# RWKV chain: block-diagonal keys instead of block-diagonal states, one state updated in place, w2/a2 products ordered by kind, v transposed on the full array

## The chip, the cores and the metric

The kernel runs on one core of one Trainium2 chip. The core has a matrix engine (TensorE, PE in the profile, with its weight loads as PEld), a vector engine (DVE), a scalar engine (ACT), GpSimd (POOL) and a queue engine (SP) that issues most DMAs. Each engine works through its own instructions in order and waits on semaphores for the others. The metric is device time in microseconds, a median of runs of one launch.

## The reference, cut to what matters

The model has two layers of a first kind on 256 tokens and 256 context tokens, and one hybrid layer. Each layer of the first kind holds an RWKV branch, a convolution branch, gates, and a product-key expert layer. The change lies in the RWKV branch, which for 16 heads of width 64 and both directions computes

```
def step(S, inp):                       # S: 64x64 state of a head
    w_t, k_t, v_t, kk_t, a_t = inp[:5]
    sa = jnp.einsum('bhvk,bhk->bhv', S, kk_t)
    S = (S * w_t[:, :, None, :] - sa[..., None] * (kk_t * a_t)[:, :, None, :]
         + v_t[..., None] * k_t[:, :, None, :])
    y = jnp.einsum('bhvk,bhk->bhv', S, inp[5]) if emit else None
    return S, y
```

with decay `w` from `tanh(w1) @ w2[d]` and `a` from `a1 @ a2[d]`, where w2 and a2 have 64 rows for each direction d. In layer 0 outputs are wanted for all 512 tokens; in layer 1 only for the 256 that aren't context.

## The kernel before, in words

Activations lie channels by tokens; a pair of heads fills the 128 partitions. Each layer walks over 8 pairs, 16 in all. For a pair, `rwkv_a` projects k, r and v (128 channels x 512 tokens), forms the w2 and a2 products of both directions (weights 64 x 128, tile `w2` with direction 0 in partitions 0 to 63 and direction 1 in 64 to 127; L432 and L437), scans the decay, and builds for each of 8 chunks of 64 tokens the chunk matrices (`scps`, L485), the transposed keys (`btps`, L499) and the tile `uv`, whose upper 64 partitions hold the chunk's v with tokens on partitions (`vps`, L509, and its copies, L511). `rwkv_inv` inverts the chunks' triangular matrices, mostly on DVE, with 32x32 matmuls (L678, L684 in layer 0; L742 to L772 in layer 1).

`rwkv_b` is the chain: 8 steps for each direction, one chunk a step. A step is `bp` (L571, plus L573 with the state `zb` and the keys `krp`), two copies of its head blocks to `bs` (L578, one on DVE, one on ACT), `up` (L580), two copies to `uv` (L582), `zp` (L585), and the new state: ACT scales the old state by `pcs` into the other of two buffers (L589), and DVE adds `zp`, head block by head block (L592). States are block-diagonal, 64x64 for each head; the keys are written twice side by side by a copy on GpSimd (L569), so that one product serves both heads. Outputs `yp` (L557) are one product with the state and, a step later, one with `uv`.

The instruction order on each engine is not the program's order: a scheduler at build time, with priorities and a cost model of its own, sorts the instructions, and fills the chain's gaps on PE with independent projections (`zbps`, `zaps`, `gtps`, `zps`, L258, and `adaps`, L279), as the table `PLAN` hands them out. The work of pair j in `rwkv_a` and the chain of pair j-1 run interleaved. PSUM tiles of the tag `rk` come from two buffers, which the w2 and a2 products, `scps`, `btps` and `vps` share.

## Time and profile before

| | before |
|---|---|
| median of 3 runs | 5218.21 us (5210.64 to 5221.29) |
| profiled execution, device time | 5211.48 us |
| its span, first to last instruction | 5209.7 us |
| PE busy | 4967.9 us, 95% |
| DVE busy | 3488.0 us, 67% |
| ACT busy | 2561.0 us, 49% |
| POOL busy | 182.2 us, 3% |
| chain that ended last | PE 74%, ACT 12%, DVE 8%, DMA 3% |

The pairs of layer 0 run from about 90 to 1010 us of the span, those of layer 1 from about 2930 to 3640 us; the change touches nothing outside them. A PE record counts as busy until its modelled end, so short waits between matmuls are hidden in the busy share; they show as the distance between starts. An fp32 matmul leaves two records (two passes), a PE transpose one.

### The profile page before, as it was taken

Reading aid. Unit: us, or ns where it says so; the run is one execution under the profiler, and the core shown is the slowest. Engines: PE = TensorE matmul, PEld = TensorE weight load, DVE = VectorE, ACT = ScalarE, POOL = GpSimd, SP = SyncE. Lnnn points to the kernel's source line nnn. Section 1 sums busy time; section 2 is a strip of 40 time slices with the busy share of each in tenths; the row PEclk is TensorE's granted clock in tenths of the full one; section 3 lists DMA queues with packets and bytes.
Section 4 is the critical chain, followed back from the end, with each engine's and each line's share of the span. In section 5 each row is a group of like instructions: output and inputs, shape, how many; then the busy total and the mean of one; then the engine's idle time right before and its main releaser. Section 6 shows DMA issues by size and latency. Waiting matters only on the chain.

```text
span 5209.7 us, 86462 instructions
## 1 busy us (share of the span) xinstructions
PE 4967.9 (95%) x33298; PEld 4170.8 (80%) x33298; DVE 3488.0 (67%) x7830; ACT 2561.0 (49%) x4754; POOL 182.2 (3%) x409
## 2 busy tenths in 40 slices
PE   8999998999999999999999999998899999989989
PEld 6677776678777888888887787877889999987888
DVE  4888878558995455555555566656796777765654
ACT  4345444534989322222223445445478544455564
POOL 0000001000000000000000010101000000000000
PEclk9999999999999999999999899888999999999999
DMA  4332323543444644444442332323656877733544
GB/s 137 107 91 88 90 81 93 167 151 101 160 171 163 234 144 142 142 143 142 143 146 70 111 84 78 85 61 92 210 187 222 279 227 238 226 116 118 167 131 146
DMA packets 432974, 740.50 MB, mean 142 GB/s; under 512 B 132210, under 2 KB 273202, under 8 KB 427826
## 3 DMA queue, kind: packets, MB, share of 16 engines
q1 hardware_dynamic: 431042, 732.29, 44.1%
q8 instruction: 262, 4.29, 0.3%
q10 hardware_dynamic: 1520, 2.69, 0.1%
q14 instruction: 150, 1.23, 0.1%
HBM read 622.37 MB, written 112.49 MB: 141 GB/s over the span
## 4 chain that ended last, share of the span: by engine, by line
PE 74%; ACT 12%; DVE 8%; DMA 3%; issue 2%; SPq 0%; ACTq 0%; POOL 0%; DVEq 0%; POOLq 0%
PE v L1180 20%; PE s L258 14%; PE zps L258 5%; ACT ws L1126 3%; PE adaps L279 3%; PE qps L258 2%; PE ops L258 2%; PE gtps L258 2%; ACT pt L1121 2%; PE ops L1368 2%; ACT whi L238 2%; ACT pt L1120 2%; PE bp L571 1%; DVE wlo L240 1%; PE zbps L258 1%
## 5 line engine op out<-in xcount | busy, mean ns | idle before, releaser
L258 PE MATMUL s<-h,whi 128*128 128x512 f32 (+1 forms) x4096 | 1058.7, 343 | 1.3 <-ACT whi L238 0.7
L240 DVE TENSOR_TENSOR wlo<-wraw,whi 128x1024 fp32r<-128x1024 f32 (+2 forms) x602 | 724.7, 1205 | 470.9 <-ACT whi L238 458.4
L238 ACT CAST whi<-wraw 128x1024 fp32r<-128x1024 f32 (+2 forms) x602 | 621.9, 1034 | 727.0 <-PE s L258 200.0
L258 PEld LDWEIGHTS s<-h,whi 128*128 128x128 f32 x4096 | 703.8, 191 | 68.6 <-ACT ge L1136 1.0
L258 PE MATMUL s<-h,wlo 128*128 128x512 f32 (+1 forms) x2048 | 704.2, 344 | 9.1 <-DVE wlo L240 9.1
L1180 PE MATMUL v<-al,vh 128*128 128x512 f32 (+1 forms) x2048 | 689.7, 337 | 0.6 <-DVE al L953 0.6
L1180 PE MATMUL v<-ah,vl 128*128 128x512 f32 (+1 forms) x2048 | 689.2, 337 | 0.0
L1180 PE MATMUL v<-ah,vh 128*128 128x512 f32 (+1 forms) x2048 | 682.7, 338 | 2.1 <-ACT ah L952 1.5
L952 ACT CAST vh<-vraw 128x1024 fp32r<-128x1024 f32 x256 | 261.9, 1050 | 719.2 <-PE v L1180 574.9
L1226 DVE SCALAR_TENSOR_TENSOR x<-v,mod,x 128x256 f32<-128x256 f32 x768 | 333.7, 477 | 272.6 <-PE v L1180 272.1
L1180 PEld LDWEIGHTS v<-ah,vh 128*128 128x128 f32 x2048 | 387.3, 190 | 49.7 <-ACT ah L952 9.4
L1180 PEld LDWEIGHTS v<-al,vh 128*128 128x128 f32 x2048 | 388.8, 190 | 46.3 <-DVE al L953 4.8
L258 PEld LDWEIGHTS s<-h,wlo 128*128 128x128 f32 x2048 | 390.3, 191 | 44.4 <-DVE wlo L240 10.3
L1180 PEld LDWEIGHTS v<-ah,vl 128*128 128x128 f32 x2048 | 388.1, 190 | 40.3 <-issue 1.4
L953 DVE TENSOR_TENSOR vl<-vraw,vh 128x1024 fp32r<-128x1024 f32 x256 | 308.6, 1220 | 98.9 <-ACT vh L952 98.9
L258 PE MATMUL zps<-h,whi 128*128 128x512 f32 (+3 forms) x896 | 293.6, 407 | 15.5 <-DVE lz L363 7.5
L1125 PEld LDWEIGHTS wps<-qt,pt 128*128 128x128 f32 x1536 | 215.8, 190 | 109.5 <-ACT pt L1121 91.2
L1125 PE MATMUL wps<-qt,pt 128*128 128x128 f32 x1536 | 272.3, 292 | 22.2 <-ACT pt L1121 13.6
L1126 ACT COPY ws<-wps 128x512 f32<-128x512 f32 x192 | 210.5, 1097 | 5.7 <-PE wps L1125 5.2
L258 PEld LDWEIGHTS zps<-h,whi 128*128 128x128 f32 (+1 forms) x896 | 167.5, 198 | 52.8 <-issue 16.6
L279 PE MATMUL adaps<-adaw,cs 128*2 128x128 f32 x1536 | 202.0, 274 | 5.4 <-DMA adaw<-ada 3.2
L1121 ACT ACTIVATE pt<-pt,tr,tr 128x128 f32<-128x128 f32 x384 | 180.4, 489 | 2.5
(614 smaller groups left out, 9617.4 us busy)
## 6 DMA issues: line engine op xcount, KB each, us to landing
wraw<-peu SPq DMA_DIRECT2D x256, 512.0 KB, 4.2
vraw<-pev SPq DMA_DIRECT2D x256, 512.0 KB, 4.5
wraw<-win SPq DMA_DIRECT2D x139, 512.0 KB, 3.6
adaw<-ada SPq DMA_DIRECT2D x96, 512.0 KB, 3.6
wd<-ws SPq DMA_DIRECT2D x24, 2048.0 KB, 6.8
wt<-wd SPq DMA_DIRECT2D x32, 1024.0 KB, 6.8
wraw<-w_q SPq DMA_DIRECT2D x32, 512.0 KB, 3.7
gd<-ge SPq DMA_DIRECT2D x64, 256.0 KB, 2.1
```

The costliest lines, as they stand in the source:

```text
L238: nc.scalar.copy(hi, raw)
L240: nc.vector.tensor_sub(lo, raw, hi.bitcast(F32))
L258: nc.tensor.matmul(out, w[wi][:, k, :], a[ai][:, k, ts], start=n == 0, stop=n == 3 * ko - 1)
L279: nc.tensor.matmul(ps[0:2, i * P:i * P + P], self.cs[:, k, :], w[:, k, :], start=k == 0, stop=k == KO - 1)
L952: self.nc.scalar.copy(hi, src)
L953: self.nc.vector.tensor_sub(lo, src, hi.bitcast(F32))
L1120: nc.scalar.activation(pt, self.iota, AF.Abs, bias=tr[3][:, cs])
L1121: nc.scalar.activation(pt, pt, AF.Relu, bias=tr[2][:, cs], scale=tr[4][:, cs])
L1125: nc.tensor.matmul(ps[:, t, :], pt, qt[:, t1 + t], start=True, stop=True)
L1126: nc.scalar.copy(ws[:, :, t0 + t1:t0 + t1 + 4].rearrange("p i t -> p t i"), ps)
L1180: nc.tensor.matmul(ps[:, m, :], va[i][wi][:, ms], aa[i][ai], start=n == 0, stop=n == 3 * GI - 1)
L1226: nc.vector.scalar_tensor_tensor(x[:, k, ts], src[:, m, ts], self.mod[l][:, 40 + k, s:s + 1], x[:, k, ts], op0=ALU.mult, op1=ALU.add)
```

## The change

Four edits, in `rwkv_a` and `rwkv_b`:

- The two w2 products (directions 0 and 1) are written one after the other, then their two activations, then the same for a2. Before it was w2, a2 of direction 0, then of direction 1.
- v is transposed with four 128x128 transposes into one PSUM tile, two chunks in each, instead of eight products of 64 columns into two tiles. Four copies to `uv` remain, each of 64 x 512 elements.
- `krp` is now block-diagonal and holds keys and receptances (2 x 2 x 64). Two GpSimd copies a step and direction write it (one for each head) instead of one. Both `bp` and the output product read it.
- The state is a full 128x128 tile, one for each direction, whose off-diagonal blocks are never read into a result. ACT scales it in place, and DVE adds `zp` in one instruction of 128x128 instead of two of 64x64.

```diff
--- before.py
+++ after.py
@@ -426,18 +426,16 @@
         pcs = rp.tile([P, 2, 8], F32, tag="pcs", name="pcs", bufs=2)
         t65 = lambda name: rp.tile([P, 8, 65], F32, tag="t65", name=name, bufs=2)
         lds, ths, bes = [], [], []
-        for d in range(2):
-            ds = slice(64 * d, 64 * d + 64)
-            ps = pr.tile([P, 512], F32, tag="rk", name="wps")
-            nc.tensor.matmul(ps, w2[ds, 0], self.tw[ds], start=True, stop=True)
-            ld = tl("ld")
-            nc.scalar.activation(ld, ps, AF.Tanh, scale=0.5, bias=self.w0h[:, d, j:j + 1])
-            lds.append(ld)
-            ps = pr.tile([P, 512], F32, tag="rk", name="aps")
-            nc.tensor.matmul(ps, w2[ds, 1], self.za[ds], start=True, stop=True)
-            th = tl("th")
-            nc.scalar.activation(th, ps, AF.Tanh, scale=0.5, bias=self.a0h[:, d, j:j + 1])
-            ths.append(th)
+
+        for q, (src, bias, res, name) in enumerate(((self.tw, self.w0h, lds, "ld"), (self.za, self.a0h, ths, "th"))):
+            pss = [pr.tile([P, 512], F32, tag="rk", name=("wps", "aps")[q]) for _ in range(2)]
+            for d in range(2):
+                ds = slice(64 * d, 64 * d + 64)
+                nc.tensor.matmul(pss[d], w2[ds, q], src[ds], start=True, stop=True)
+            for d in range(2):
+                t = tl(name)
+                nc.scalar.activation(t, pss[d], AF.Tanh, scale=0.5, bias=bias[:, d, j:j + 1])
+                res.append(t)
         self.pop("z")
         for d in range(2):
             ld, th = lds[d], ths[d]
@@ -503,12 +501,13 @@
             nc.gpsimd.memset(uv[0:64], 0.0)
             UV.append(uv)
         self.pop("t")
-        for c0 in range(0, 8, 4):
-            ps = pr.tile([P, 4, P], F32, tag="rk", name="vps")
-            for c in range(4):
-                nc.tensor.matmul(ps[64:128, c, :], v[:, (c0 + c) * 64:(c0 + c) * 64 + 64], self.ident, start=True, stop=True)
-            for d in range(2):
-                nc.scalar.copy(UV[d][64:128, c0:c0 + 4, :], ps[64:128])
+
+        ps = pr.tile([P, 4, P], F32, tag="rk", name="vps")
+        for c in range(4):
+            nc.tensor.transpose(ps[:, c, :], v[:, c * P:c * P + P], self.ident)
+        for d in range(2):
+            for e in range(2):
+                nc.scalar.copy(UV[d].rearrange("p (c e) m -> p c e m", e=2)[64:128, :, e], ps[64 * e:64 * e + 64])
         bo = tl("bo", "bo", 2)
         nc.vector.tensor_add(bo[:, :Tr], kds[0][:, :Tr], kds[1][:, :Tr])
         nc.vector.scalar_tensor_tensor(bo[:, :Tr], bo[:, :Tr], self.par(l, "r_k", j), r[:, :Tr], op0=ALU.mult,
@@ -534,11 +533,13 @@
         if self.bs is None:
             tiles = lambda name, n: [[rp.tile([P, P], F32, name=f"{name}{d}{i}", bufs=1) for i in range(n)] for d in range(2)]
 
-            self.bs, self.zb, self.krp = tiles("bs", 1), tiles("zb", 2), tiles("krp", 1)
+
+
+            self.bs, self.zb = tiles("bs", 1), tiles("zb", 1)
+            self.krp = [rp.tile([P, 2, 2, 64], F32, name=f"krp{d}", bufs=1) for d in range(2)]
             for d in range(2):
                 nc.gpsimd.memset(self.bs[d][0][64:128], 0.0)
-                for t in self.zb[d]:
-                    nc.gpsimd.memset(t, 0.0)
+                nc.gpsimd.memset(self.krp[d], 0.0)
         oT = rp.tile([P, T2], F32, tag="oT", name="oT", bufs=1)
 
 
@@ -565,14 +566,15 @@
                 Z = Zs[d]
                 bp = ch(d, "bp")
                 if i:
-                    krp = self.krp[d][0]
-                    nc.gpsimd.tensor_copy(krp.rearrange("p (h t) -> p h t", h=2),
-                                          KR[d][:, 0, c * 64:c * 64 + 64].unsqueeze(1).to_broadcast([P, 2, 64]))
+                    krp = self.krp[d]
+                    n = 2 if emit(c) else 1
+                    for hh, hs in enumerate(heads):
+                        nc.gpsimd.tensor_copy(krp[hs, 0:n, hh], KR[d][hs, 0:n, c * 64:c * 64 + 64])
                 nc.tensor.matmul(bp, SC[d](c, 0), UV[d][:, c, :], start=True, stop=i == 0)
                 if i:
-                    nc.tensor.matmul(bp, krp, Z, start=False, stop=True)
+                    nc.tensor.matmul(bp, krp[:, 0].rearrange("p h t -> p (h t)"), Z, start=False, stop=True)
                     if emit(c):
-                        output(c, Z, KR[d][:, 1, c * 64:c * 64 + 64].unsqueeze(1).to_broadcast([P, 2, 64]))
+                        output(c, Z, krp[:, 1])
                 bs = self.bs[d][0]
                 for hh, hs in enumerate(heads):
                     copy[hh](bs[0:64, hs], bp[hs, hs])
@@ -583,15 +585,13 @@
                 if i < 7 or l == 0:
                     zp = ch(d, "zp")
                     nc.tensor.matmul(zp, BT[d][:, c, :], UV[d][:, c, :], start=True, stop=True)
-                    zn = self.zb[d][i % 2]
+                    zn = self.zb[d][0]
                     pc = pcs[:, d, c:c + 1]
                     if i:
                         nc.scalar.activation(zn, Z, AF.Copy, scale=pc)
-                    for hs in heads:
-                        if i:
-                            nc.vector.scalar_tensor_tensor(zn[hs, hs], zp[hs, hs], pc[hs], zn[hs, hs], op0=ALU.mult, op1=ALU.add)
-                        else:
-                            nc.vector.tensor_scalar(zn[hs, hs], zp[hs, hs], pc[hs], None, op0=ALU.mult)
+                        nc.vector.scalar_tensor_tensor(zn, zp, pc, zn, op0=ALU.mult, op1=ALU.add)
+                    else:
+                        nc.vector.tensor_scalar(zn, zp, pc, None, op0=ALU.mult)
                     Zs[d] = zn
                 if late[d]:
                     output(*late[d])
```

What the scheduler makes of it, at three places. First PE at the front of the second pair of layer 0, where the w2 products are `wps<-tw` and the a2 products `aps<-za`, direction 0 before direction 1. Before:

```order
L417 MATMUL ssps<-sq,blk 128x512
L432 MATMUL wps<-tw,w_1359 128x512
L580 MATMUL up<-bs_1815,sc 128x128
L437 MATMUL aps<-za,w_1359 128x512
L432 MATMUL wps<-tw,w_1359 128x512
L571 MATMUL bp<-uv,sc 128x128
L258 MATMUL gtps<-h_119,wlo 128x512
```

Now:

```order
L417 MATMUL ssps<-sq,blk 128x512
L434 MATMUL wps<-tw,w_1354 128x512
L582 MATMUL up<-bs_1805,sc 128x128
L434 MATMUL wps<-tw,w_1354 128x512
L434 MATMUL aps<-za,w_1354 128x512
L573 MATMUL bp<-uv,sc 128x128
```

The second w2 product has moved ahead of the first a2 product. Before, the adjacent pair was a2 of direction 0 with w2 of direction 1; now it is w2 of direction 1 with a2 of direction 0. Over the 16 pairs, products of opposite directions stood next to each other 10 times before, and do 8 times now.

Second PE in the chain that runs beside the third pair of layer 0; the two directions are told apart by the buffers of `bs` and of `zb` and `krp`. Before:

```order
L580 MATMUL up<-bs_1815,sc 128x128
L279 MATMUL adaps<-adaw,cs 2x128
L571 MATMUL bp<-uv,sc 128x128
L573 MATMUL bp<-zb_1820,krp_1822 128x128
L585 MATMUL zp<-uv,bt 128x128
L557 MATMUL yp<-kr,zb_1820 128x128
L557 MATMUL yp<-sc,uv 128x128
L580 MATMUL up<-bs_1816,sc 128x128
```

Now:

```order
L573 MATMUL bp<-uv,sc 128x128
L575 MATMUL bp<-zb_1807,krp_1809 128x128
L558 MATMUL yp<-krp_1809,zb_1807 128x128
L558 MATMUL yp<-sc,uv 128x128
L573 MATMUL bp<-uv,sc 128x128
L575 MATMUL bp<-zb_1808,krp_1810 128x128
L582 MATMUL up<-bs_1805,sc 128x128
L558 MATMUL yp<-krp_1810,zb_1808 128x128
L558 MATMUL yp<-sc,uv 128x128
L582 MATMUL up<-bs_1806,sc 128x128
L279 MATMUL adaps<-adaw,cs 2x128
L587 MATMUL zp<-uv,bt 128x128
```

Before, the directions took turns half a step apart: `bp` of one stood beside `zp` of the other. Now they go in step, both `bp`, both `up`, both `zp`.

Third ACT at the same place, with the in-place scale `zb<-zb`. Before:

```order
L578 COPY bs_1815<-bp 64x64
L582 COPY uv<-up 64x64
L578 COPY bs_1816<-bp 64x64
L589 ACTIVATE zb_1817<-zb_1818,pcs 128x128
L582 COPY uv<-up 64x64
```

Now:

```order
L591 ACTIVATE zb_1807<-zb_1807,pcs 128x128
L580 COPY bs_1805<-bp 64x64
L580 COPY bs_1806<-bp 64x64
L591 ACTIVATE zb_1808<-zb_1808,pcs 128x128
L584 COPY uv<-up 64x64 x2
```

The scale of direction 0 now stands ahead of the copy to `bs`, and that of direction 1 ahead of both copies to `uv`; being in place, each waits for the output product that reads the state. ACT also loads its function tables 125 times in the whole program now, 113 before; 10 of the 12 more stand among the decay's activations of layer 1, at L420 (rn) and L437 (ld, th).

## Rows read from the trace of the kernel before

**Rows 1.** First part of the page: busy time, share of the span, instructions.
```profile
PE 4967.9 (95%) x33298; PEld 4170.8 (80%) x33298; DVE 3488.0 (67%) x7830; ACT 2561.0 (49%) x4754; POOL 182.2 (3%) x409
```

**Rows 2.** Busy time by stretch; last columns PE clock, DMA share, GB/s.
```profile
200.00:800.00 600.00, 586.00 (x3896) 434.91 (x3895) 489.71 (x1283) 288.74 (x617) 55.89 (x135) 0.99 0.30 89
800.00:1010.00 210.00, 188.70 (x1154) 134.70 (x1153) 150.25 (x361) 107.38 (x224) 25.32 (x40) 0.93 0.35 109
2930.00:3500.00 570.00, 551.23 (x5742) 459.69 (x5741) 367.33 (x1009) 274.47 (x629) 58.56 (x140) 0.89 0.29 81
```

**Rows 3.** Groups by line and shape: the products that transpose v.
```profile
L509 PE MATMUL vps<-ident,v 128*64 128x128 f32 x256 | 34.8, 279 | 1.1 <-ACT bt L500 1.1
```

**Rows 4.** Timeline of PE, layer 0: start, duration, instruction, records merged.
```profile
253.19 1.09 PE L509 MATMUL vps<-ident,v 128*64 128x128 f32 x8
254.21 0.49 PE L557 MATMUL yp<-sc,uv 128*128 128x128 f32 x2
```

**Rows 5.** Timeline of PE, layer 0: four transposes among chain matmuls.
```profile
327.76 0.39 PE L573 MATMUL bp<-zb,krp 128*128 128x128 f32 x2
327.98 0.61 PE L499 MATMUL btps<-ident,be 128*128 128x128 f32 x4
328.43 0.39 PE L557 MATMUL yp<-kr,zb 128*128 128x128 f32 x2
```

**Rows 6.** Timeline of PE, first pair: a2 and w2 products, adjacent and alone.
```profile
94.50 0.69 PE L437 MATMUL aps<-za,w 64*128 64x512 f32 x1
94.50 0.69 PE L432 MATMUL wps<-tw,w 64*128 64x512 f32 x1
...
95.56 0.50 PE L258 MATMUL zbps<-h,wlo 128*128 128x512 f32 x1
...
98.50 1.12 PE L437 MATMUL aps<-za,w 64*128 64x512 f32 x2
```

**Rows 7.** Timeline of all engines, one chain step of layer 0.
```profile
331.46 0.39 PE L573 MATMUL bp<-zb,krp 128*128 128x128 f32 x2
...
332.19 0.21 ACT L578 COPY bs<-bp 64x64 f32<-64x64 f32 x1 [0.75 <-DVE bs L578]
...
332.45 0.49 PE L580 MATMUL up<-bs,sc 128*128 128x128 f32 x2
...
333.22 0.21 ACT L582 COPY uv<-up 64x64 f32<-64x64 f32 x1
...
333.72 0.39 PE L585 MATMUL zp<-uv,bt 128*128 128x128 f32 x2
...
334.17 0.58 DVE L592 SCALAR_TENSOR_TENSOR zb<-zp,pcs,zb 64x64 f32<-64x64 f32 x2
...
335.54 0.39 PE L573 MATMUL bp<-zb,krp 128*128 128x128 f32 x2
```

**Rows 8.** Groups by line and shape: state update, a wider update, the scale.
```profile
L592 DVE SCALAR_TENSOR_TENSOR zb<-zp,pcs,zb 64x64 f32<-64x64 f32 x416 | 117.5, 282 | 41.9 <-PE zp L585 32.3
L1226 DVE SCALAR_TENSOR_TENSOR x<-v,mod,x 128x256 f32<-128x256 f32 x768 | 333.7, 477 | 272.6 <-PE v L1180 272.1
L589 ACT ACTIVATE zb<-zb,pcs 128x128 f32<-128x128 f32 x208 | 82.8, 401 | 133.7 <-DVE zb L592 126.6 <-DVE zb L594 3.3 <-DVE tm L720 2.6
```

**Rows 9.** Waits of PE, 800 to 1010 us: total us, times, longest.
```profile
PE bp L571 <- DVE zb L592: 9.1, 9, 2.7
```

**Rows 10.** Groups of ACT: table loads in the decay (count, busy, mean ns).
```profile
L439 ACT ACT_TABLE_LOAD x10 | 12.8, 1283 | 0.2
```

**Rows 11.** The GpSimd key copy: durations (min/median/max), and its group.
```profile
L569 POOL COPY krp<-kr x224: 288/293/1266, 101.7 to 3621.8; 128x128 f32<-128x128 f32 x112
...
L569 POOL COPY krp<-kr 128x128 f32<-128x128 f32 x224 | 87.7, 391 | 633.0 <-PE bp L573 628.4 <-DMA am<-inv 2.9 <-DVE kr L464 1.8
```

**Rows 12.** Busy time by stretch around the inversion of a layer-1 pair.
```profile
3214.00:3220.00 6.00, 5.09 (x261) 4.53 (x259) 1.87 (x4) 2.79 (x9) 0.09 (x1) 1.00 0.02 5
3220.00:3226.00 6.00, 6.00 (x96) 5.23 (x97) 3.19 (x8) 2.28 (x4) 0.86 (x1) 0.54 0.01 3
```

## The prediction

> **What bounds the kernel now.** I read the page's first part, then the busy time by stretch, then PE's timeline inside a stretch. PE is busy 95% of the span [rows 1], and 586 of 600 us while layer 0's pairs run, 551 of 570 in layer 1's [rows 2]; only the last chain of layer 0, where projections run out, leaves 21 of 210 us open. DVE is next with 490 of 600. So in these stretches PE work that goes away shortens the kernel about one for one, DVE, ACT and POOL work only where PE waits for it. The busy share hides short waits, though: in the chain the reader must look at the distance between starts. A chain step goes from the `bp` product at 331.46 to that direction's next at 335.54, 4.08 us, and the directions share it [rows 7]. Matmuls back to back start 0.22 us apart (327.76 to 327.98, [rows 5]). In a step PE has 12 chain products and two fillers, 14 x 0.22 = 3.1 us; the other 1.0 us of the step is waiting that no view shows as idle.
>
> **v transposed on the full array.** 256 records of `vps` [rows 3] are 128 products in 32 groups of four. A group holds PE from 253.19 to 254.21, 1.02 us [rows 4]: 32 x 1.02 = 32.6 us. The four transposes that take the place of two groups hold it from 327.98 to 328.43, 0.45 us [rows 5], with the same shape and fp32: 16 x 0.45 = 7.2 us. The copies to `uv` keep their number and size. Saved: 25.4 us of PE; 27 if the slower start of a narrow group counts too, 0 if PE were to wait there anyway, which 97% busy excludes nearly. I take 25.4. This is the surest term.
>
> **w2 and a2 side by side.** The a2 product of direction 0 and the w2 product of direction 1 both start at 94.50 and the next matmul starts at 95.56: two in 1.06 us, as long as one alone (98.50, 1.12 us) [rows 6]. The two halves of the array do run at once, if nothing stands between. But the instruction order has only 8 such neighbours now, 10 before, because the shared PSUM buffers hold the second product back and the scheduler puts projections between. The edit costs 2 x 1.06 = 2.1 us instead of gaining. The Trainium skill, TensorEngine Tiling (Array Packing), Key Properties, says that tiles on different rows of the array can load weights and multiply in parallel; the trace agrees, with the two starts at 94.50. By that rule alone the edit would look like a gain for all 32 pairs of products. The order says otherwise. Bounds: were all 32 pairs overlapped, 22 x 1.06 = 23 us gained; were none, 10.6 lost.
>
> **Table loads.** Ten more loads in layer 1 at 1.283 us [rows 10], with two elsewhere 15.4 us of ACT. ACT is busy 274 of 570 us there and PE has projections ahead while the decay is built, so most is covered: between 0 and +15.4, I take +2, since PE is 97% busy at that place.
>
> **The chain.** One update of 128x128 replaces two of 64x64. Two cost 0.58 us (334.17, [rows 7]); one with 64 columns is 0.282, one with 256 is 0.477 [rows 8], so 128 columns lie near 0.35. DVE is freed of some 208 x 0.22 = 46 us, and the new state is there 0.22 us sooner. Against it, ACT's scale now waits for the output product that reads the state, and the copies queue behind it. I walk a step of the new order with the old distances, from `bp` of direction 0 (time 0). Its output product starts at 0.22, the other direction's second `bp` product at 0.89. The scale starts 0.43 behind the output product (0.39 long, [rows 5]), 0.65, and is done at 1.05 (0.40, [rows 8]). The `bs` copy on ACT could start at 0.73 (331.46 to 332.19) and now starts at 1.05; `up` follows 0.26 later, 1.31; ACT's `uv` copy 0.77 after that, 2.08, but the other scale, behind an output product at 1.53, holds ACT until 2.36. `zp` starts 0.26 later, 2.62 (as `up` after its copy); DVE's update 0.45 later, 3.07, done 3.42; `bp` at 3.49 and its second product at 3.81 [rows 7]. So 3.81 against 4.08 us: the gain of 0.22 a direction is partly eaten by the scale, and going in step saves a little more. I use 0.27 a step.
> Where does it count? In layer 0 seven chains run beside a next pair; their first four steps go at the pace of [rows 7], the other four have projections and the inversion's DVE work between, where I count half: 7 x 4 x 0.27 + 7 x 4 x 0.135 = 11.3 us. In chains without cover PE waits for the state, 9 times for 9.1 us [rows 9], and about as often in the last chain of layer 1; 17 waits x 0.22 = 3.7 us. Layer 1's other chains have projections in each gap: nothing. Sum 15.0 us. Bounds: 128 steps x 0.27 = 35 us gained; or both scales (0.40 each) on the path with only one update's 0.22 saved, 0.36 x 56 = 20 us lost.
> The doubled key copies are hidden: each waits for the output product's end (about 0.65 into the step) and takes 2 x 0.293 us, done near 1.3 of 3.8; POOL waited 628 us for `bp` over 224 copies, 2.8 us each [rows 11].
>
> **Sum.** -25.4 + 2.1 + 2.0 - 15.0 = -36.3 us from the profiled execution's 5211.5, 5175. That execution was 6.7 us quicker than the median of the runs shown; I put half of this back: 5178 us.
>
> **The rivals.**
> Chain gains nothing: the step stays at 4.08 because the scale waits, and only the transposes count: 5211.5 - 25.4 + 2.1 + 2.0 = 5190, with half the offset 5193. For it: `bs` and `uv` copies stand behind a scale in ACT's order. Against it: the walk, even with 0.40 for each scale.
> The clock: around a layer-1 inversion PE runs at 2.4 GHz while busy 5.09 of 6 us with 261 small matmuls, and then shows 0.54, close to the 1.2 GHz level [rows 12]; over layer 1's stretch the mean is 0.89 [rows 2], so 22% of 570 = 125 us at the low level. In six of the eight inversions of layer 1 the new order puts 2 to 4 us of chain and projection matmuls among the 32x32 products, where 0.7 us stood before. If that keeps the clock up half of that time, 125/2/2 = 31 us more are gained: 5147. Against it: the last products of an inversion stay together, so I don't count on it; it may also go the other way by some 20 us.
> Slower, contention of GpSimd with DVE: the key copies have a median of 0.293 but a mean of 0.391 and a longest of 1.266 us [rows 11], so they do wait for somebody. If each of the 224 added copies held DVE for 0.293 us in the chain, that is 65 us, and with DVE in order ahead of `bs`, `uv` and the state it would all land on PE: 5178 + 65 = 5243. It decides from 36.3/224 = 0.16 us an added copy. Against it: DVE is 82% busy and loses 46 us of own work; update and copy need not meet. The Trainium skill, SBUF — State Buffer, "SBUF: two separate sides", has such a rule: GpSimd and a DVE instruction with two SBUF inputs share one port pair, and whoever comes first blocks the other for its whole length. The longest copy, 1.266 us, fits it on POOL's side; no row here shows how far DVE is held.
> Side by side works after all: if neighbours with a wait between still overlap, 23 us more, 5155.
>
> **How the numbers follow.** Forecast 5178: 0.58, its own range 5160 to 5200. Chain gains nothing, 5193: 0.17. Clock, 5147: 0.13. Slower by GpSimd, around 5240: 0.07. Side by side, 5155: 0.02; the rest, near 5210, 0.03. A measurement of this kernel can tell 0.2%, 10 us, from no change; measured against 5218, faster means below 5208. The forecast, the clock, the side by side and most of the second case lie below: 0.86. Within 10 us lie the upper end of the second case and the rest: 0.08. Slower: 0.06. The range 5140 to 5207 leaves out the slower rival and the ends of the clock's case, and takes in the chain's bound of 35 us and its loss up to the size of the other terms.
>
> **What would show it.** `vps` in 64 records holding PE some 7 us instead of 33. Starts of a direction's `bp` 3.7 to 3.9 us apart in layer 0's first four steps. The state update at 0.34 to 0.36 us, in half as many instructions. Two-row-half products starting together in only 8 places. DVE busy some 45 us less, POOL some 65 more. PE's busy time in the two layers' stretches less by 20 to 30 us, at much the same share. Wrong would be: steps of 4.1 us or more with ACT's scale named as what PE waited for; key copies that `bp` waits for; or a clock in layer 1 far from 0.89.

## The result, and the profile after

The changed kernel took 5158.43 us (median of 4 runs, 5150.37 to 5167.87) against 5214.86 us for the kernel before in the same comparison (4 runs): a ratio of 0.9891, 95% interval 0.9874 to 0.9907. That is 56 us faster; the forecast was 5178, 40 us below the median shown to it. The profiled execution took 5154.13 us, 57 us less than that of before.

The first part of the page, which answers to [rows 1]:

```profile
PE 4915.5 (95%) x33106; PEld 4129.6 (80%) x33106; DVE 3428.0 (67%) x7590; ACT 2565.2 (50%) x4766; POOL 246.2 (5%) x629
```

PE is still the bound at the same share, and lost 52 us of busy time; DVE lost 60, POOL gained 64. To see where the time went I cut both traces at the same events: from the first `ssps` product (L417) of a layer's second pair to that of its eighth, six pairs of each layer. Before, layer 0 and then layer 1; columns as in [rows 2]:

```profile
192.53:827.67 635.14, 621.08 (x4145) 460.98 (x4143) 519.67 (x1343) 309.57 (x647) 56.68 (x138) 0.99 0.30 88
2964.62:3503.12 538.50, 522.07 (x5307) 435.29 (x5306) 352.66 (x983) 264.08 (x611) 58.12 (x138) 0.89 0.28 79
```

After:

```profile
190.32:805.74 615.42, 602.32 (x4074) 447.09 (x4071) 494.39 (x1246) 303.45 (x647) 79.22 (x222) 1.00 0.31 91
2938.91:3454.08 515.17, 500.34 (x5233) 415.00 (x5232) 332.24 (x898) 276.54 (x622) 79.41 (x222) 0.94 0.29 83
```

Layer 0's six pairs are 19.7 us shorter, layer 1's 23.3. The granted clock of layer 1 rose from 0.89 to 0.94: 118 us of 538 at the 1.2 GHz level became 62 of 515 (twice the missing share times the length). The forecast's terms for six pairs of layer 1 are 6 x (2.04 - 0.45) = 9.5 us of transposes and nothing for the chain. Cut from a layer's first `ssps` to the first `ya` product (L258) behind its last chain, layer 0 went from 944.3 to 918.3 us and layer 1 from 790.4 to 759.6: nearly the whole gain lies there.

The groups that answer to [rows 3], [rows 8] and [rows 11]:

```profile
L572 POOL COPY krp<-kr 64x128 f32<-64x128 f32 x352 | 125.5, 356 | 368.4 <-PE yp L558 309.2 <-PE bp L575 32.7 <-issue 10.3
L591 ACT ACTIVATE zb<-zb,pcs 128x128 f32<-128x128 f32 x208 | 82.9, 401 | 125.4 <-DVE bs L580 67.7 <-PE yp L558 36.0 <-PE bp L575 16.6
L592 DVE SCALAR_TENSOR_TENSOR zb<-zp,pcs,zb 128x128 f32<-128x128 f32 x208 | 71.7, 347 | 55.2 <-PE zp L587 54.2
L507 PE MATMUL vps<-ident,v 128*128 128x128 f32 x64 | 10.2, 280 | 0.0
```

One update of 128x128 takes 0.347 us where two took 0.58. The scale now waits for the output product `yp` too (36.0 us), and so do the key copies (309 us), as the walk had them. `vps` has 64 records; a group of four holds PE 0.41 to 0.49 us (one of the 16 groups is split).

A chain step that answers to [rows 7], in layer 0's third pair:

```profile
329.76 0.39 PE L575 MATMUL bp<-zb,krp 128*128 128x128 f32 x2
...
330.40 0.40 ACT L591 ACTIVATE zb<-zb,pcs 128x128 f32<-128x128 f32 x1 [2.17 <-DVE bs L580]
...
330.71 0.19 ACT L580 COPY bs<-bp 64x64 f32<-64x64 f32 x1
...
330.96 0.49 PE L582 MATMUL up<-bs,sc 128*128 128x128 f32 x2
...
332.06 0.38 PE L279 MATMUL adaps<-adaw,cs 128*2 128x128 f32 x2
...
332.37 0.49 PE L587 MATMUL zp<-uv,bt 128*128 128x128 f32 x2
332.42 0.21 ACT L584 COPY uv<-up 64x64 f32<-64x64 f32 x1 [0.21 <-DVE uv L584]
332.79 0.38 PE L279 MATMUL adaps<-adaw,cs 128*2 128x128 f32 x2
332.90 0.35 DVE L592 SCALAR_TENSOR_TENSOR zb<-zp,pcs,zb 128x128 f32<-128x128 f32 x1 [0.51 <-PE zp L587]
333.10 0.49 PE L587 MATMUL zp<-uv,bt 128*128 128x128 f32 x2
...
333.52 0.38 PE L279 MATMUL adaps<-adaw,cs 128*2 128x128 f32 x2
...
333.82 0.49 PE L573 MATMUL bp<-uv,sc 128*128 128x128 f32 x2
...
334.15 0.39 PE L575 MATMUL bp<-zb,krp 128*128 128x128 f32 x2
```

From `bp` to `bp` it is 4.39 us, not 3.81, and not even 4.08. Up to the new state the walk holds: `up` starts after 1.20 us (forecast 1.31), `zp` after 2.61 (2.62), and the update is done after 3.49 (3.42). Then the step's next `bp` product should have followed 0.07 us later, and it starts at 333.82, 0.57 us later. Three fillers (independent projections, here `adaps`) stand in the step where two stood before. They are not hidden in waits: the `uv` copy at 332.42 is done at 332.63, and the other direction's `zp` starts only at 333.10, behind the filler that PE took at 332.79; one more filler stands before `bp`.

Less 0.22 for each filler, the step is 3.73 us; before it was 4.08 - 0.44 = 3.64. This is rough: in the step shown the product behind a filler starts 0.30 or 0.31 us after it. Layer 0's steps at 2.4 GHz with the same number of chain products and fillers take about the same time before and now: with 13 and 1, 3.81 and 3.78 us; with 12 and 4, 4.52 and 4.60; with 12 and 5, 4.8 and 4.8 (medians of 3 to 12 steps). Over the whole chain it is no better. Six steps of this pair run from 325.24 to 351.63, 26.4 us with 20 fillers among them; before, from 327.76 to 353.18, 25.4 us with 16:

```profile
325.24 0.39 PE L575 MATMUL bp<-zb,krp 128*128 128x128 f32 x2
...
351.63 0.39 PE L575 MATMUL bp<-zb,krp 128*128 128x128 f32 x2
```

```profile
353.18 0.39 PE L573 MATMUL bp<-zb,krp 128*128 128x128 f32 x2
```

What changed around layer 1's inversion is seen by stretches of 6 us from the first 32x32 product of the fourth pair's, against [rows 12] for the same pair before:

```profile
3173.20:3179.20 6.00, 6.00 (x213) 5.61 (x212) 1.46 (x6) 2.43 (x8) 0.86 (x4) 1.00 0.02 5
3179.20:3185.20 6.00, 5.95 (x156) 5.20 (x156) 4.06 (x10) 5.17 (x12) 0.94 (x1) 0.91 0.01 3
3185.20:3191.20 6.00, 6.00 (x58) 5.32 (x57) 3.06 (x6) 0.99 (x3) 0.94 (x1) 0.52 0.29 90
```

Before, PE waited 0.9 of the first 6 us and ran the second 6 us at 0.54. Now it is busy in both, because products of the previous pair's chain stand among the small ones, and the low level comes almost wholly in the third stretch. In the records of PE's products (two for each), 4 to 6 others stood between the first and the last small product of each layer-1 inversion before; now it is 16 to 26 in the six middle ones, 4 still in the first and the last.

### The profile page after: what moved, and what is told of

Same layout as the page of the kernel before. It is cut to its first block, busy times and chain, and to the rows that moved or that the text cites. A ratio compares the mean times of both kernels' runs of the same rounds, so it can differ in the third digit from the quotient of the medians.

```text
span 5152.3 us, 85900 instructions
## 1 busy us (share of the span) xinstructions
PE 4915.5 (95%) x33106; PEld 4129.6 (80%) x33106; DVE 3428.0 (67%) x7590; ACT 2565.2 (50%) x4766; POOL 246.2 (5%) x629
## 4 chain that ended last, share of the span: by engine, by line
PE 73%; ACT 12%; DVE 9%; DMA 3%; issue 2%; POOL 0%; ACTq 0%; SPq 0%; DVEq 0%; POOLq 0%
PE v L1180 20%; PE s L258 14%; PE zps L258 5%; ACT ws L1126 3%; PE adaps L279 2%; PE gtps L258 2%; PE ops L258 2%; PE qps L258 2%; ACT pt L1121 2%; PE ops L1368 2%; DVE wlo L240 2%; ACT whi L238 2%; ACT pt L1120 2%; PE yp L558 1%; PE up L582 1%
## 5 line engine op out<-in xcount | busy, mean ns | idle before, releaser
L258 PE MATMUL s<-h,whi 128*128 128x512 f32 (+1 forms) x4096 | 1059.0, 343 | 1.3 <-ACT whi L238 0.7
L258 PEld LDWEIGHTS s<-h,whi 128*128 128x128 f32 x4096 | 704.1, 191 | 68.8 <-ACT ge L1136 1.0
L258 PE MATMUL s<-h,wlo 128*128 128x512 f32 (+1 forms) x2048 | 704.3, 344 | 9.3 <-DVE wlo L240 9.3
L258 PEld LDWEIGHTS s<-h,wlo 128*128 128x128 f32 x2048 | 390.4, 191 | 44.1 <-DVE wlo L240 10.3
L258 PE MATMUL zps<-h,whi 128*128 128x512 f32 (+3 forms) x896 | 292.8, 404 | 18.9 <-DVE lz L363 7.5
L1125 PE MATMUL wps<-qt,pt 128*128 128x128 f32 x1536 | 272.5, 292 | 22.1 <-ACT pt L1121 13.7
L258 PEld LDWEIGHTS zps<-h,whi 128*128 128x128 f32 (+1 forms) x896 | 167.6, 196 | 60.1 <-issue 19.4
```

The source lines that it names most:

```text
L258: nc.tensor.matmul(out, w[wi][:, k, :], a[ai][:, k, ts], start=n == 0, stop=n == 3 * ko - 1)
L1125: nc.tensor.matmul(ps[:, t, :], pt, qt[:, t1 + t], start=True, stop=True)
```

## The experiments

Each was timed in alternation with the kernel before on the same chip; ratios are to that. "L0" and "L1" are the six middle pairs of each layer in its profile, cut as above.

| kernel | median us | ratio (95%) | L0 us | L1 us | L1 clock |
|---|---|---|---|---|---|
| before | 5211 to 5216 | 1 | 635.1 | 538.5 | 0.89 |
| transposes alone (e1) | 5169.68 | 0.9916 (0.9899 to 0.9932) | 625.1 | 512.6 | 0.95 |
| w2/a2 alone (e2) | 5210.65 | 0.9999 (0.9986 to 1.0012) | 630.8 | 542.5 | 0.88 |
| chain alone (e3) | 5215.12 | 1.0007 (0.9995 to 1.0019) | 622.2 | 554.9 | 0.90 |
| changed, update in halves (e5) | 5225.51 | 1.0024 (1.0014 to 1.0035) | 623.4 | 538.2 | 0.91 |
| before, covered inversion (e9) | 5229.07 | 1.0032 (1.0017 to 1.0047) | 633.8 | 537.3 | 0.95 |
| changed, covered inversion (e10) | 5188.38 | 0.9964 (0.9950 to 0.9979) | 618.4 | 536.0 | 0.96 |
| changed, no scale (e6) | 5182.84 | 0.9950 (0.9932 to 0.9969) | 626.4 | 520.1 | 0.92 |
| changed, fillers later (e11) | 5175.83 | 0.9934 (0.9911 to 0.9956) | 618.9 | 521.9 | 0.92 |
| changed again (e12) | 5155.77 | 0.9893 (0.9871 to 0.9914) | 616.2 | 515.0 | 0.94 |
| transposes and w2/a2 (e8) | 5174.18 | 0.9922 (0.9900 to 0.9945) | 625.2 | 513.5 | 0.94 |
| transposes and chain (e7) | 5158.83 | 0.9897 (0.9876 to 0.9919) | 618.6 | 516.8 | 0.94 |
| changed, last state left out (e13) | 5162.34 | 0.9904 (0.9884 to 0.9923) | 609.4 | 514.9 | 0.94 |

**The parts one at a time.** Theory A: less PE work and a shorter chain. Theory B: a good part of the gain is the clock in layer 1. The first kernel takes the transposes alone:

```diff
-                nc.tensor.matmul(ps[64:128, c, :], v[:, (c0 + c) * 64:(c0 + c) * 64 + 64], self.ident, ...)
+            nc.tensor.transpose(ps[:, c, :], v[:, c * P:c * P + P], self.ident)
```

> The kernel before with the transposes of v alone. Theory A (PE work and chain latency): 32 groups of 1.02 us become 16 of 0.45, about 25 us less, some 5190 us. Theory B (the clock gives half of the whole gain): also 25 us less for the work, and more or less only by what the time at the low clock differs; half a us for each us at 1.2 GHz more or less (344 us in the whole trace of before, leaving out the first 90 us).

```profile
192.09:817.18 625.09, 612.97 (x4073) 455.30 (x4071) 517.95 (x1343) 310.05 (x647) 55.77 (x138) 0.98 0.30 90
2947.84:3460.42 512.58, 499.97 (x5234) 409.71 (x5232) 352.69 (x984) 279.12 (x623) 63.18 (x138) 0.95 0.30 84
```

42 us, where 25 is all the PE time that the transposes can free. Layer 0 gave 10.0 us in six pairs, close to the 9.5 worked out; layer 1 gave 25.9, with the clock at 0.95. From 90 us on, its trace has 299 us at the low level where the one before had 344; half of these 45 us is 22, and 25 and 22 are 47, near the measured 42. So theory B holds here. In this run too, 18 to 24 other records stand among the small products of the six middle inversions of layer 1. The second takes the order of w2 and a2 alone (`for q in ...: for d in ...`):

> The kernel before with the w2/a2 products alone in the new order. Both theories: no gain; 0 to 4 us slower, since neighbours from both halves of the array don't get more, and the decay's activations load tables more often. A rival (the products overlap although others stand between): 20 us faster, 5195.

No difference. Nor does the edit change how many of these products run side by side: eight pairs of them start together in this run, as in the kernel before. The third takes the chain's edits alone (the two copies into a block-diagonal `krp`, one `zb`, one update, of which the last is shown):

```diff
-                    for hs in heads:
-                            nc.vector.scalar_tensor_tensor(zn[hs, hs], zp[hs, hs], pc[hs], zn[hs, hs], ...)
+                        nc.vector.scalar_tensor_tensor(zn, zp, pc, zn, op0=ALU.mult, op1=ALU.add)
```

> The kernel before with the chain's edits alone (block-diagonal keys, one state in place, one update). Theory A: the step gets shorter, 15 us less, 5200. Theory B: the step itself gains nothing (in the trace after, the first steps of a layer-0 chain take 4.39 us against 4.08), and what is gained comes from the new order, which leaves fewer us at 1.2 GHz: 20 to 30 us less with 40 to 60 us fewer at the low clock, and within 5 us of before if the low-clock time stays near 344 us.

```profile
193.24:815.41 622.17, 611.90 (x4146) 453.12 (x4144) 494.23 (x1246) 302.81 (x647) 82.07 (x222) 1.00 0.31 90
2948.37:3503.24 554.87, 532.14 (x5305) 438.25 (x5304) 335.78 (x900) 276.62 (x623) 78.28 (x222) 0.90 0.27 77
```

No difference in all, and so theory B's second case: 357 us at the low level, against 344. In the profile 13.0 us are gained in layer 0 and 16.4 lost in layer 1, with the same instructions and about the same clock. Why layer 1 loses isn't settled; the profiled execution took 5227.78 us, 12.7 more than this kernel's median, so part of the loss may belong to that execution. Only 4 to 6 other records stand among the small products of its inversions, as before: it is the transposes that let the chain in there. The fourth is the changed kernel with the update again in two halves:

```diff
-                        nc.vector.scalar_tensor_tensor(zn, zp, pc, zn, op0=ALU.mult, op1=ALU.add)
+                        for hs in heads:
+                            nc.vector.scalar_tensor_tensor(zn[hs, hs], zp[hs, hs], pc[hs], zn[hs, hs], op0=ALU.mult, op1=ALU.add)
```

> The changed kernel, but DVE updates the state in two instructions of 64x64 again (208 x 0.22 us more on DVE, 0.22 us later in each step). Theory A: 10 to 15 us slower than the changed kernel, some 5172. Theory B: within 5 us of it, apart from half of any difference in the time at the low clock.

```profile
192.87:816.26 623.39, 605.13 (x4073) 446.57 (x4071) 517.10 (x1342) 303.87 (x647) 79.91 (x222) 1.00 0.30 90
2961.53:3499.75 538.22, 517.32 (x5233) 423.26 (x5232) 354.98 (x982) 272.89 (x619) 82.30 (x222) 0.91 0.28 80
```

67 us slower than the changed kernel, a miss for both theories. Cost of the halves, at most 0.22 us for each of 208 updates, is 46 us if all of it were on the path. PE's order differs as well: the scheduler prices two updates otherwise and places fillers anew. Steps of layer 0 with 12 chain products and 4 fillers take 4.66 us against 4.60 in the changed kernel, but most steps now hold four fillers where most held three. The low level took 357 us of the trace against 272, which at half is 43 us. So this run changes the order, the clock and the update at once; it doesn't price the update.

**The clock by itself.** To the kernel before, products that nothing reads are added among the small ones (the first of four places is shown). Each has 64 columns of weights and 512 columns of data, so it covers half of the array's columns, not the full array as the expectation has it:

```diff
+        cover = lambda ps: nc.tensor.matmul(ps.rearrange("p u t -> p (u t)")[64:128], self.reset[:, 0:64], self.reset[:, 0:512], ...)
...
             for u in range(16):
+                if u in (4, 12):
+                    cover(q1[d])
...
```

> The kernel before, with 12 added products in each inversion of layer 1 (and of the hybrid layer): full-array bf16 products of constants into PSUM partitions that nothing reads, spread evenly among the 192 small 32x32 products. The result is unchanged. In the traces so far an inversion of layer 1 with 3 to 4 other products among its small ones is followed by 14 to 20 us at 1.2 GHz, one with 11 to 20 chain products among them by 3 to 14 us. Theory 'clock' (it is the full-array work among the small products that keeps the clock up): low time in layer 1's pairs falls from 196 to 110 to 140 us, which gives back about half of the difference, 28 to 43 us, against 8 x 12 x 0.21 = 20 us of added products; 5190 to 5207 against 5212. Rival 'shorter work' (the low time falls only because transposing v leaves less to do, the order is no cause): low time stays at 185 to 205 us and the products cost their 20 us: 5232.

```profile
2965.26:3502.58 537.32, 526.61 (x5380) 423.58 (x5378) 352.67 (x983) 264.65 (x611) 59.01 (x138) 0.95 0.29 80
```

Timeline of PE in it, one added product and the block of small ones behind it, and the first three stretches of 6 us of that inversion:

```profile
3219.32 0.40 PE L734 MATMUL q<-reset 128*64 128x512 bf16 x1
3219.66 0.69 PE L746 MATMUL q<-xl,sc 32*32 32x32 f32 x32
```

```profile
3217.00:3223.00 6.00, 6.00 (x213) 4.35 (x213) 1.10 (x2) 1.16 (x3) 0.00 (x0) 1.00 0.01 3
3223.00:3229.00 6.00, 6.00 (x137) 4.36 (x131) 3.06 (x7) 3.77 (x8) 0.94 (x1) 1.00 0.01 3
3229.00:3235.00 6.00, 6.00 (x74) 4.26 (x72) 2.99 (x5) 1.68 (x4) 0.00 (x0) 0.65 0.01 3
```

The second stretch, at 0.54 before [rows 12], is at 1.00; the low level comes only in the third, at 0.65, and over six pairs it fell from 118 to 54 us. So larger products among the small ones do hold the clock up, in an otherwise unchanged kernel. They also fill PE's waits inside the inversion (0.9 to 1.5 us each before, 0.0 now), and this run doesn't tell the two apart. Fewer waits alone don't do it: in the run of the chain alone the fifth and the eighth inversion wait 0.35 and 0.0 us with 4 other records among their products, and 13.7 and 23.9 of the 30 us from their first small product are at the low level. The time is another matter: an added product holds PE 0.34 us (3219.32 to 3219.66), not 0.21. 72 of them are 24 us, and the six pairs came out 1.2 us shorter: 64 us at the low level gave back some 25 us, 0.4 us each. The whole kernel is 18 us slower. So the low time came out as theory 'clock' had it (122 us in layer 1's eight pairs) and the time as its rival had it (5232, inside the interval of 5220 to 5236), because the added products cost more than 0.21 us each. The profiled execution, 5218.14 us, was one of this kernel's quickest, with a mean clock of 0.973 where the median of its 12 runs is 0.970 (0.965 before). The same added to the changed kernel:

> The changed kernel with the same 12 full-array products in each inversion. Theory 'clock': low time in layer 1's pairs falls from 134 to about 90 us, the first and the last inversion (4 and 2 other products among them so far) gaining most; 22 us given back against 20 us of added products: 5146 to 5166, about the changed kernel's 5158. Rival 'shorter work': low time stays near 134 and the products cost 20 us: 5178.

30 us slower than the changed kernel, a miss for both times: most inversions had their cover already. In layer 1's eight pairs 106 us are at the low level, where the theory had about 90 and the changed kernel has 134. In the six pairs the low level fell only from 61 to 48 us by the clock's records, and 72 products of 0.34 us are 24 us; the pairs are 20.9 us longer.

**The order by itself.** One row of the table of fillers is altered in the changed kernel; the work is the same.

```diff
-{'z': 'G', 'c0': 'G', 'c1': 'AA', 'c2': 'C'}
+{'z': 'G', 'c3': 'G', 'c4': 'AA', 'c5': 'C'}
```

> The changed kernel with one row of the filler table altered: in layer 1's middle pairs the projections are handed out at the chain's steps 3, 4 and 5 instead of 0, 1 and 2. No work is added or left out. By its instruction order 16 to 20 other products then stand among the small products of each of layer 1's middle inversions, where 13 to 20 stood. Theory 'clock': low time in layer 1 falls a little further, from 134 to 115 to 130 us, 5145 to 5158. Rival 'shorter work': no difference, 5158 within 8; a time above 5168 would say that the fillers are missed at the chain's first steps.

```profile
2942.11:3464.05 521.94, 507.97 (x5234) 421.74 (x5233) 331.43 (x900) 280.08 (x625) 81.70 (x222) 0.92 0.30 82
```

About as many other records stand among the small products of the six middle inversions as in the changed kernel (18 to 21 against 16 to 26), and yet the clock fell to 0.92: 79 us low against 61, by the clock's records before they are rounded. The count is therefore not all that decides; in these inversions PE also waits longer between products, 0.6 to 1.7 us where the changed kernel's six waited 0.0 to 0.7. The six pairs are 6.8 us longer with the same instructions, 0.4 us for each of 17 us more at the low level. The whole kernel is 17 us slower than the changed one, a miss for both theories. The expectation read more than 5168 as fillers missed at the chain's first steps, but PE is idle no longer than in the changed kernel, 14.0 us of the six pairs against 14.8.

**The chain's scale.** Here the state is kept unscaled and ACT's scaling is left out:

```diff
...
-                        nc.gpsimd.tensor_copy(krp[hs, 0:n, hh], KR[d][hs, 0:n, c * 64:c * 64 + 64])
+                        nc.gpsimd.tensor_scalar(krp[hs, 0:n, hh], KR[d][hs, 0:n, c * 64:c * 64 + 64], pcl[d][hs], None, op0=ALU.mult)
...
-                        nc.scalar.activation(zn, Z, AF.Copy, scale=pc)
-                        nc.vector.scalar_tensor_tensor(zn, zp, pc, zn, op0=ALU.mult, op1=ALU.add)
+                        nc.vector.scalar_tensor_tensor(zn, zn, pcl[d], zp, op0=ALU.mult, op1=ALU.add)
```

> The changed kernel without ACT's scaling of the state: the state is kept unscaled, DVE multiplies and adds in its one update, and the GpSimd copies of keys and receptances multiply by the decay instead of only copying. Theory 'the scale holds the chain' (my walk: the bs copy waits behind a scale of 0.40 us in ACT's queue, twice a step): a step of layer 0's chain falls from 4.39 us by 0.3 us or more, PE's waits for bs and uv copies go, 5130 to 5150. Rival 'PE's own products hold the chain' (15 products a step, three of them fillers): the step stays within 0.1 us of 4.39 and the time at 5150 to 5165; more than 5170 would say that GpSimd's copies have come onto the path.

```profile
541.43 0.39 PE L576 MATMUL bp<-zb,krp 128*128 128x128 f32 x2
...
542.42 0.49 PE L583 MATMUL up<-bs,sc 128*128 128x128 f32 x2
...
543.46 0.49 PE L588 MATMUL zp<-uv,bt 128*128 128x128 f32 x2
...
544.73 0.39 PE L576 MATMUL bp<-zb,krp 128*128 128x128 f32 x2
```

```profile
187.74:814.12 626.38, 605.79 (x4074) 456.13 (x4072) 496.20 (x1246) 278.24 (x563) 136.52 (x222) 0.98 0.31 89
2948.53:3468.67 520.14, 506.42 (x5234) 420.03 (x5232) 331.60 (x898) 255.90 (x550) 129.60 (x222) 0.92 0.29 82
```

The step, one of layer 0's fifth pair, is 3.30 us with no filler in it; the changed kernel's, less its fillers, was 3.73. From `bp` to `up` it is 0.99 us where the changed kernel's step has 1.20, and from `up` to `zp` 1.04 where it has 1.41 (a filler stands in these 1.41). So the scale does stand on the step's path, before the copies to `bs` and to `uv`, with 0.2 us at the first and some 0.4 in all as an estimate. And the kernel is 24 us slower than the changed one. The expectation read a time above 5170 as GpSimd's work coming onto the path; PE's waits in the six pairs of each layer name no GpSimd operation. A shorter step gave fillers other places, and layer 0 lost 11 us, layer 1 five, with 27 us at the low level in layer 0 against 3 and 82 in layer 1 against 61. The step's length is not what this kernel pays for.

**The parts in pairs.** The last four ran side by side.

> The changed kernel itself, nothing altered, on the same chip as the next three, so that parts can be told apart by less than the difference between chips. 5150 to 5168, a ratio of 0.987 to 0.991 against before.

> The kernel before with v's transposes and the w2/a2 order, without the chain's edits: what is missing against the changed kernel is the chain. Theory 'the chain gives what the walk says, but only beside the transposes' (the walk's 15 us; layer 0's stretch was 10 us shorter in the changed kernel than with the transposes alone): 5168 to 5180, all of it in layer 0's pairs. Rival 'the chain gives nothing' (the chain's edits alone measured 1.0007): within 5 us of the changed kernel.

Without the chain's edits it is 18 us slower, the edge of what can be told (intervals 0.9871 to 0.9914 and 0.9900 to 0.9945). Layer 0's six pairs, one by one, without the chain's edits:

```profile
189.25:288.29 99.04, 95.44 (x663) 71.50 (x661) 84.79 (x221) 50.47 (x108) 8.84 (x23) 1.00 0.31 90
288.29:391.52 103.23, 101.28 (x683) 75.31 (x682) 87.17 (x226) 51.70 (x109) 9.19 (x23) 1.00 0.31 91
391.52:498.25 106.73, 104.37 (x684) 77.23 (x682) 86.44 (x225) 52.05 (x109) 9.25 (x23) 0.97 0.30 88
498.25:600.72 102.47, 101.56 (x683) 75.38 (x682) 86.20 (x223) 51.77 (x109) 9.60 (x23) 1.00 0.31 92
600.72:709.16 108.44, 105.93 (x684) 78.35 (x683) 86.62 (x226) 52.06 (x109) 9.30 (x23) 0.95 0.30 87
709.16:814.41 105.25, 104.49 (x683) 77.57 (x682) 86.75 (x224) 51.77 (x108) 9.60 (x23) 0.97 0.30 90
```

and the fourth of the six in the changed kernel:

```profile
498.12:600.63 102.51, 101.01 (x683) 74.93 (x682) 82.81 (x209) 50.76 (x109) 13.01 (x37) 1.00 0.31 92
```

This pair, at 2.4 GHz throughout, takes 102.5 us with the chain's edits and without them. What the edits add in layer 0 is that no later pair falls to the low level (pairs at 0.97 and 0.95 take 105.3 to 108.4). Beside the old transposes they do give something: there a pair at 2.4 GHz takes 105.2 us, and 104.2 with the chain's edits alone (the kernel before, then e3):

```profile
399.44:504.61 105.17, 103.36 (x695) 76.67 (x694) 86.98 (x225) 51.97 (x109) 9.57 (x23) 1.00 0.31 90
```

```profile
607.04:711.21 104.17, 102.79 (x696) 76.13 (x695) 82.67 (x209) 50.73 (x109) 13.06 (x37) 1.00 0.30 91
```

> The changed kernel with the w2 and a2 products in the old order: two neighbouring pairs of half-array products more, table loads as before. Forecast's terms (2.1 us of PE and 2 us of table loads): 4 us quicker than the changed kernel, which the measurement can hardly tell. Rival 'the edit is worth nothing' (alone it measured 0.9999): no difference. More than 12 us either way would say that the order of the rest has changed with it.

No difference from the changed kernel: w2 and a2 side by side are worth nothing either way.

> The changed kernel without the last state of each direction in layer 0: zp, scale and update of step 7, which nothing reads, as layer 1 leaves them out already. The result is unchanged. It saves 8 chains x 2 products x 0.22 us of PE, 3.5 us, and two scales and two updates at each chain's end. If PE's work sets layer 0's pace: 3 to 6 us quicker than the changed kernel. Rival 'covered': no difference, since other work stands there. Slower only if the order of the rest changes.

```diff
-                if i < 7 or l == 0:
+                if i < 7:
```

Six pairs of layer 0 are 6.0 us shorter than in the changed kernel, but its eighth, which stands alone, took 209 us to the first `ya` product instead of 201, with 37 us at the low level instead of 24; no gain in all. No version ran faster than the changed kernel.

## Why the prediction was right, and where its steps were not

The direction and most of the size were right: PE was the bound, and PE time that went away shortened the kernel: its busy time fell by 18.8 us in layer 0's six pairs and by 21.7 in layer 1's. Only 9.5 us of each is the transposes' work; the rest is the same records taking less time, while the time at the low level fell from 17 to 3 us in layer 0 and from 118 to 62 in layer 1. As an estimate, the transposes' 25 us and half of what the low time fell over the whole trace (from 90 us on, 344 us before and 272 now) make 61 us; the profiled execution is 57 us shorter. For the transposes alone, transposes and w2/a2, fillers later and no scale the same sum gives 48, 44, 41 and 31 us, and their profiled executions gained 39, 34, 41 and 31, within 10 us of it. It fails for the update in halves (19 gained by the sum, 13 lost) and is 10 us off for the chain alone.

The measured 5158 lies 20 us below the forecast, just outside its own range of 5160 to 5200, and that it came so near is in part luck: the chain's 15 us didn't come as a shorter step, and the clock, put at nothing, gave at least as much (17 us in the run of the transposes alone, and half of 72 us by the sum above). Of the forecast's signs of being wrong, a clock in layer 1 far from 0.89 came (0.94), and half of another: steps of more than 4.1 us, but PE's waits don't name the scale. Term by term:

- **Transposes, -25.4 us.** The work is as predicted (64 records, 0.41 to 0.49 us a group) and came off one for one or better in layer 0. But the term was too small: alone it measured -42 us. In the new order chain products of the previous pair fall among layer 1's small products, and PE spends less time at 1.2 GHz. (Probably the scheduler finds the next inversion ready sooner when `vps` is short; that was not tried.) That is the rival that had 0.13 and 31 us more; in this run it came at about half that size, on top of the work. The prediction didn't count on it because the last products of an inversion stay together. They do, and a low stretch follows them still (the third, at 0.52), but it starts later and is shorter.
- **w2/a2, +2.1, and table loads, +2.** Nothing measurable, alone or beside the rest. In the profile two pairs of such products start together, where eight did before and eight were forecast. The edit isn't what changed this: eight pairs start together with it alone, and two in the changed kernel with the old order. The loads are there, and PE waits for the activation behind them in few places (layer 1's six pairs; total us, times, longest):

```profile
PE aps L434 <- ACT ld L437: 3.4, 3, 1.8
```

- **Chain, -15.0.** The size is about what the edits are worth beside the transposes (18 us), the reason is not. Steps were to take 3.81 us and took 4.39. The walk failed between the update and the next `bp`, 0.07 us in it and 0.57 measured, where it took fillers as hidden behind the chain's waits: PE follows an order fixed at build, and a filler ahead of a ready product delays it (the other direction's `zp` by some 0.4 us: it starts 0.47 us after its `uv` copy, and 0.06 in the step without fillers of the run without the scale). The bound of 20 us lost is also added up wrongly: 0.80 - 0.22 is 0.58 us a step, 32 us. Beside the transposes the edits are worth nothing in an undisturbed pair; without them 1 us a pair, and nothing in the whole kernel. What they changed is the order, and by it the clock in layer 0 and the length of layer 1's last pair (144.2 us from its `ssps` to the first `ya` product; 151.9 with the transposes and w2/a2 alone, with 35 and 41 us at the low level). That the order does this is shown by the runs; by which property of the order isn't.
- **Contention of GpSimd with DVE.** Did not come: DVE lost 60 us where 45 were forecast, and one update stayed at 0.347 us. The longest key copy took 1.857 us. The Trainium skill, SBUF — State Buffer, "SBUF: two separate sides", has GpSimd and DVE lock each other out of a shared port pair, where the DVE instruction is in a two-port mode or reads two inputs from SBUF; the state update takes `zp` from PSUM. The long copies fit it on GpSimd's side, and no run here shows DVE held. With copies of 0.70 us instead of 0.36 (the run without the scale) the update still took 0.344 us.

What a microsecond at the low level costs was the forecast's other number, half. Over the six middle pairs of layer 1 in the twelve kernels without added products (72 pairs), the time of a pair follows the line 81.4 us + 0.46 for each us at the low level (correlation 0.81). The kernel with fillers moved gives 0.4, the covered one 0.4. Between the kernel before and the changed one it is less: 23.3 us, of which 9.5 are the transposes' work, for 57 us at the low level, 0.24. The Trainium skill, TensorE: Matmul & The Clock Gate, Terms, takes the loss as the low time times one less the granted share, which is half here; layer 1's rows come to half or less.

## What to carry to other kernels

When a build-time scheduler sets the order, an edit is priced twice: by the work it takes off the bound, and by the order it leaves; here the second moved the time by 17 us with the same work (the row of fillers), and with the update's own price it moved it by 67 us where one update became two. Compare stretches cut at the same events, with their granted clock, before believing a walk of one step. Removed work that lets two phases overlap can be worth more than its own time (42 us for 25 here), and a shorter dependent step can be worth nothing while the engine has other work in a fixed order.

## What the runs showed of the hardware

- In these traces PE falls to 1.2 GHz after runs of 32x32 products although it is nearly always busy (6.00 of 6 us at 0.54, [rows 12]). With 12 products of 128x64 weights by 512 columns added among them the same stretch stayed at 2.4 GHz, 1.00, and the next one was at 0.65; an added product held PE 0.34 us.
- A GpSimd multiply by a per-partition scalar took 0.70 us for 64x128 fp32 where a copy took 0.36:

```profile
L573 POOL TENSOR_SCALAR krp<-kr,pcs 64x128 f32<-64x128 f32 x352 | 246.4, 700 | 271.3 <-PE yp L558 221.2 <-PE bp L576 21.2 <-issue 4.8
```
